# The last norm, gate and output of a fused layer: squares, splits and factors placed sooner, weight remainders read from DRAM, gate operands two steps ahead

## The chip, the cores and the metric

The kernel runs on one core of a Trainium2 chip. The core has five engines that run side by side, each through its own list of instructions in a fixed order: PE (TensorE, the matmuls), DVE (VectorE), ACT (ScalarE), POOL (GpSimd) and SP (SyncE, which here only issues DMAs). The engines wait for each other by semaphores. The metric is the device time of one execution in microseconds, lower is better. Three executions of the kernel before took 2519.19, 2524.06 and 2526.34 us, median 2524.06.

## The reference

One layer on 2048 prompt tokens and 64 further tokens, width 1024, all in float32. What matters for this change is its end; `x` is the layer's input and `p` a side input of width 256:

```python
merged = sigmoid(gA) * yA + sigmoid(gB) * yB
out = einsum('btd,de->bte', merged, w_o)
x = x + rms_norm(out, g_post)
gate = sigmoid(einsum('btd,de->bte', rms_norm(x, g_ple), w_ple_gate))
x = x + einsum('btp,pd->btd', p, w_ple_proj) * gate
```

`rms_norm(x, g)` is `x * rsqrt(mean(x*x) + 1e-6) * g`, the mean over the 1024 features of one token. Everything ahead of it (the input projections, a short convolution, a chunked recurrence) is not touched.

## The kernel before, in words

**Numbers.** A float32 product is made of three matmuls in a rounded format: each operand is split into a high part (a cast, on ACT) and a remainder (a subtraction, on DVE), and PE adds high x high, high x remainder and remainder x high. `split` (L229) is that pair for an activation; `split_w` (L269) does it for a weight tile of 128x512 that SP has loaded (L240). A weight's remainder is the same for every block of tokens, so `split_w` stores it in DRAM the first time and later only loads it (L280, 256 KB, in place of the subtraction); the argument `anew` names the parts that are split again all the same.

**Blocks.** The 2112 tokens go in three blocks of 768, 704 and 640 tokens; features lie on the partitions in eight tiles (j = 0 to 7) of 128, tokens along the row. The last block is worked on in two halves of 320 tokens.

**Products in turn.** Large products of the last block are made by `in_turn` (L573): a 2 x 2 scheme with seven products in place of eight, one after the other, 48 matmuls of 128x320 each (L608, L609, L610). A product's moving operand is half of the activation or a sum of halves (its names are B11, B21, T1 to T4, B22); `operand_of` (L555) makes it from four pieces, k = 0 to 3, each with additions (L559 to L566) and a split (L230). `prepare` asks for the pieces of the next product while the current one runs. Each finished output tile goes to the stage's `sink`.

**The end phase**, which is where the change is, runs after the last product W_O. In order on PE: the seven products of W_O; the final gate of block 2 (704 tokens, W_G: its tiles j = 0 and 1 together, then j = 2 to 7, each 48 matmuls of 128x352, L645 to L647); the `ple` product of block 3 (w_ple_proj, L1313 to L1315); the gate of block 3 as `gate_in_turn` (seven products of W_G, 336 matmuls); and a tail of elementwise work and stores. Block 2's gate is kept back until then so that PE has work while block 3's `final_norm` (L1420) runs on the other engines. That norm is a chain:

- `sum_squares` (L736): eight squares on ACT (L741), summed on DVE (L742).
- `col_rstd` (L713): PE transposes the sum (L722), DVE reduces (L723) and scales (L700), POOL takes the power (L702); then PE transposes the result into rows (L710) and ACT copies it out (L733).
- for each j: scale by g_post (L1446), add `x` that a DMA has fetched (L1431, L1447), and the squares of the second norm.
- the same chain again for the second norm, then one scaling for each j (L1469), which gives the operand of `gate_in_turn`.

Where the chain's PE instructions stand among the gate's matmuls is set by a plan: `spread_out` (L1528) attaches steps of generators to places in the program (a hook after each group of matmuls), and tuples of counts say how many steps each place runs. Of `final_gate` (L1495), each j loads x and p of block 2 again (L1339, on POOL's queue), and makes sigmoid (L1506), product (L1507), sum (L1508) and a store of y (L1509, POOL's queue). Block 2's normed activation h was stored to DRAM (L1478) and is loaded again and split in W_O (`ask_h` L1480, `split_held` L1487).

**Buffers.** Row-shaped tiles (`r_...` in the profile) come from one ring; a new one waits until the last reader of the old one is through. A DMA of POOL also waits until the one eight places earlier in its list has landed.

**The middle block** (block 2 in its own turn, around 1720 to 1780 us) runs the same `final_norm`, but its PE work goes among the gate projections of block 3, and its x is stored to DRAM by POOL (L1457) for the final gate.

Of the kernel before, what the change touches and what calls it, by code (L numbers as in the profile page):

```python
# [14 lines left out]
ALU = mybir.AluOpType  # L15
# [5 lines left out]
KB = D // P  # L21
# [73 lines left out]
def hybrid_step(  # L95
# [474 lines left out]
            V.tensor_tensor(b12, b22, b12, ALU.subtract)  # L570
        return out

    def in_turn(stages, operand):  # L573

# [9 lines left out]
                made.setdefault(i, []).append(operand_of(st["raw"], st["order"][n][1], k, late))  # L584


        for k in range(2):
            prepare(1, k)
        for i, (st, n) in enumerate(todo):
            block, _, what = st["order"][n]  # L590
# [3 lines left out]
            for g in range(KH):  # L594
# [33 lines left out]
                elif what in ("p5", "p7"):  # L628
# [2 lines left out]
                        A.copy(t, ps)  # L631
                    V.tensor_tensor(p57, p57, t, ALU.add)
                    st["sink"](g, 1, 1, u2, p57)
                if i > 0:
                    prepare(i + 1, g)
                elif g < KH - 2:
                    prepare(1, g + 2)
                hook()
# [778 lines left out]
        stage["sink"] = sink  # L1417
        return stage

    def final_norm(bl, xo, acc, kept, take, early):  # L1420

        segs = bl["segs"]
        acc2, xks = None, []

        def fetch():
            j = len(xks)
            if j < KB:
                xks.append(rt())  # L1430
                paced(G.dma_start(xks[j], x_fm[j * P : (j + 1) * P, bl["t0"] : bl["t0"] + bl["n"]]))  # L1431

        for j in range(KB):
            sum_squares(j, xo[j], acc, width[0])
            if j % 2:
                yield
        for _ in range(2):
            fetch()
            yield
        rs = rt()  # L1440
        for _ in rms(acc, rs, segs):
            fetch()
            yield
        for j in range(KB):
            fetch()
            V.scalar_tensor_tensor(xo[j], xo[j], g_post[:, j : j + 1], rs, ALU.mult, ALU.mult)  # L1446
# [5 lines left out]
        stored = iter(range(0 if bl["last"] else KB))  # L1452

        def store(n):
            for i in islice(stored, n):
                kept["x", i] = spill("x", i)
                paced(G.dma_start(kept["x", i], xo[i]))  # L1457

        rs2 = rt()
        for _ in rms(acc2, rs2, segs):  # L1460
            store(2)
            yield
        ts = []
        for j in range(KB):
            store(1)
            while len(ts) < min(j + 1 + early, KB):
                i = len(ts)
                ts.append(rt())
                V.scalar_tensor_tensor(ts[i], xo[i], g_ple[:, i : i + 1], rs2, ALU.mult, ALU.mult)  # L1469
            take(j, ts[j])  # L1470
            yield
# [23 lines left out]
    def final_gate(bl, h2, kept, by_k=False):  # L1495

        segs = bl["segs"]
        for j in range(KB):
            if by_k and j < 2:
                both = gemm_by_k([W_G, W_G + 1], h2, segs, (1,)) if j == 0 else both  # L1500
                pss = both[j]
            else:
                pss = gemm(W_G + j, h2, segs, (1,) if by_k else ())
            xj, pj, t = reload(kept["x", j]), reload(kept["p", j]), rt()
            for s, ps in zip(segs, pss):
                A.activation(t[:, cols_of(s)], ps, AF.Sigmoid)  # L1506
            V.tensor_tensor(t, pj, t, ALU.mult)  # L1507
            V.tensor_tensor(t, t, xj, ALU.add)  # L1508
            G.dma_start(y_fm[j * P : (j + 1) * P, bl["t0"] : bl["t0"] + bl["n"]], t)  # L1509
            yield  # L1510

    def gate_in_turn(bl, h2, xs, kept):


        def sink(g, c, h, x, y):
# [5 lines left out]
            (V if (c, h) == (0, 1) else G).tensor_tensor(v, v, half(xs[j], h), ALU.add)  # L1521
# [148 lines left out]
    for bi, bl in enumerate(blocks):  # L1670
# [78 lines left out]
        for idx, n in in_turn(stages, a_first):  # L1749
# [2 lines left out]
                ask_rs()  # L1752
            elif nxt and (idx, n) == (W_B, 6):
                spread_out((next_ops(), (0, 1, 0, 1, 0, 1, 0) * KH))
            elif bl["last"] and idx == W_O and 1 <= n <= 4:
                run(asked, 2)
            elif bl["last"] and (idx, n) == (W_O, 5):
                a_first.clear()
                norm = sized(bl, final_norm(bl, xo, rt(), kept, lambda j, t: h2.append(t), 0))
                spread_out(  # L1760
                    (held_parts, (1,) * 4 + (2, 2)),
                    (norm, (0,) * 4 + (1,) * 4 + (2, 1, 0, 1, 1, 1, 2, 1, 2, 1, 1, 0) + (1, 1, 2, 1, 2, 1, 1)),
                    (sized(bl, ask_p()), (0,) * 16 + (1, 0, 0, 1)),
                    (sized(bl, first_halves()), (0,) * 24 + (1,) * 4),
                )
        if nxt:
            xo.extend(stages[-1]["mid"])
            fills = sized(nxt, gates(nxt, hc, kepts[bi + 1], False))
            norm = sized(bl, final_norm(bl, xo, rt(), kept, partial(split_h, h2) if first else partial(keep_h, kept), int(first)))
# [8 lines left out]
        else:  # L1778
# [55 lines left out]
```

## Time and profile before

| what | value |
|---|---|
| runs | 2519.19, 2524.06, 2526.34 us; median 2524.06 |
| profiled execution | 2522.08 us, of which the span from the first to the last instruction is 2520.4 us |
| PE busy | 2495.2 us, 99% of the span, 16254 matmuls |
| DVE, ACT, POOL busy | 1943.3 (77%), 1504.2 (60%), 530.9 us (21%) |
| DMA | 741.95 MB, mean 294 GB/s |
| end phase | gate of block 2 from 2374.19, W_G in turn from 2458.79, last matmul begins 2513.52 |

Times inside the kernel are in us from the span's start. In a row of the timeline stand the start, the duration, the engine and line, the operation with its written and read tiles, and, in brackets, how long the engine had been idle and which instruction ended that. A row of the waits names the waiting engine and line, the one it waited for, and total, count and longest. The windows give each engine's busy time within a stretch, the clock that PE was granted (1.00 is full speed) and the busy share and rate of the DMA engines. "PEld" is the loading of weights into PE, which runs beside matmuls.

### The profile page before, as it was taken

Reading aid. Unit: us, or ns where it says so; the run is one execution under the profiler, and the core shown is the slowest. Engines: PE = TensorE matmul, PEld = TensorE weight load, DVE = VectorE, ACT = ScalarE, POOL = GpSimd, SP = SyncE. Lnnn points to the kernel's source line nnn. Section 1 sums busy time; section 2 is a strip of 40 time slices with the busy share of each in tenths; the row PEclk is TensorE's granted clock in tenths of the full one; section 3 lists DMA queues with packets and bytes.
Section 4 is the critical chain, followed back from the end, with each engine's and each line's share of the span. In section 5 each row is a group of like instructions: output and inputs, shape, how many; then the busy total and the mean of one; then the engine's idle time right before and its main releaser. Section 6 shows DMA issues by size and latency. Waiting matters only on the chain. (4 is left out here: it accounts for less than half of the span.)

```text
span 2520.4 us, 47301 instructions
## 1 busy us (share of the span) xinstructions
PE 2495.2 (99%) x16254; PEld 2476.1 (98%) x16254; DVE 1943.3 (77%) x3699; ACT 1504.2 (60%) x2926; POOL 530.9 (21%) x891
## 2 busy tenths in 40 slices
PE   9999999999999999999999999999999999999998
PEld 9999999999999999999999999999999999999998
DVE  7889999988867775588885667977677776679667
ACT  6676676554554763566555555676666655566645
POOL 2032222320022021122223221002122222110133
PEclk9999999999999999999999999999999999999999
DMA  8789889997687798788889988989988879888876
GB/s 330 241 305 338 313 297 324 330 318 266 231 334 263 258 330 292 255 272 284 280 282 332 336 299 310 323 272 355 329 285 290 276 260 324 279 304 307 292 250 212
DMA packets 341937, 741.95 MB, mean 294 GB/s; under 512 B 43062, under 2 KB 48240, under 8 KB 341696
## 3 DMA queue, kind: packets, MB, share of 16 engines
q1 hardware_dynamic: 284832, 515.76, 59.1%
q0 software_dynamic: 56864, 223.16, 24.8%
q8 instruction: 128, 2.10, 0.3%
q14 instruction: 113, 0.93, 0.1%
HBM read 526.40 MB, written 212.36 MB: 293 GB/s over the span
## 5 line engine op out<-in xcount | busy, mean ns | idle before, releaser
L457 PE MATMUL pg<-r,hi 128*128 128x320 f32 (+2 forms) x3304 | 1074.7, 325 | 1.7 <-DVE r L505 1.7
L458 PE MATMUL pg<-r,hi 128*128 128x320 f32 (+2 forms) x3304 | 1066.8, 323 | 0.0
L459 PE MATMUL pg<-r,lo 128*128 128x384 f32 (+2 forms) x2380 | 775.3, 326 | 0.0
L457 PEld LDWEIGHTS pg<-r,hi 128*128 128x128 f32 x3304 | 621.0, 188 | 4.0 <-DVE r L505 2.2
L458 PEld LDWEIGHTS pg<-r,hi 128*128 128x128 f32 x3304 | 621.6, 188 | 0.0
L279 ACT CAST hi<-raw 128x512 fp32r<-128x512 f32 x550 | 339.9, 620 | 407.7 <-PE pg L458 158.8
L459 PEld LDWEIGHTS pg<-r,lo 128*128 128x128 f32 x2380 | 447.1, 188 | 0.3 <-DMA lo<-low 0.3
L230 ACT CAST hi<-raw 128x512 fp32r<-128x512 f32 x420 | 259.4, 621 | 219.8 <-PE pg L458 81.0
L609 PE MATMUL pg<-r,hi 128*128 128x320 f32 (+2 forms) x976 | 313.3, 322 | 1.6 <-DVE r L230 1.5
L608 PE MATMUL pg<-r,hi 128*128 128x320 f32 (+2 forms) x976 | 310.4, 321 | 1.4 <-ACT r L230 1.4
L459 PE MATMUL pg<-r,s 128*128 128x352 f32 (+1 forms) x924 | 291.5, 315 | 2.1 <-DMA s<-low 2.1
L230 DVE TENSOR_TENSOR lo<-raw,hi 128x512 fp32r<-128x512 f32 x320 | 219.4, 687 | 93.5 <-ACT hi L230 88.6
L230 DVE TENSOR_TENSOR r<-r,r 128x320 fp32r<-128x320 f32 (+7 forms) x374 | 221.0, 611 | 44.1 <-ACT r L230 43.3
L230 ACT CAST r<-r 128x320 fp32r<-128x320 f32 (+7 forms) x374 | 195.9, 557 | 34.1 <-DVE r L1353 8.8
L610 PE MATMUL pg<-r,lo 128*128 128x320 f32 (+2 forms) x656 | 209.2, 319 | 0.0
L609 PEld LDWEIGHTS pg<-r,hi 128*128 128x128 f32 x976 | 183.9, 189 | 4.1 <-DVE r L230 3.8
L608 PEld LDWEIGHTS pg<-r,hi 128*128 128x128 f32 x976 | 182.9, 188 | 3.3 <-ACT r L230 2.9
L230 ACT CAST hi<-s 128x512 fp32r<-128x512 f32 x164 | 101.9, 623 | 126.9 <-PE pg L458 99.0
L459 PEld LDWEIGHTS pg<-r,s 128*128 128x128 f32 x924 | 173.5, 188 | 2.4 <-DMA s<-low 2.4
L471 ACT COPY hf<-pg 128x352 f32<-128x352 f32 (+2 forms) x354 | 157.5, 448 | 0.8 <-PE pg L459 0.7
L230 DVE TENSOR_TENSOR lo<-s,hi 128x512 fp32r<-128x512 f32 x164 | 114.1, 696 | 45.0 <-ACT hi L230 40.6
L505 DVE TENSOR_TENSOR r<-hf,pg 128x128 f32<-128x128 f32 (+5 forms) x164 | 64.3, 411 | 95.7 <-PE pg L459 95.4
(391 smaller groups left out, 4239.0 us busy)
## 6 DMA issues: line engine op xcount, KB each, us to landing
raw<-w_blk SPq DMA_DIRECT2D x559, 256.0 KB, 4.5
raw<-S SPq DMA_DIRECT2D x452, 256.0 KB, 4.1
lo<-low SPq DMA_DIRECT2D x332, 256.0 KB, 4.3
s<-low SPq DMA_DIRECT2D x218, 256.0 KB, 4.9
low<-lo SPq DMA_DIRECT2D x207, 256.0 KB, 4.0
S<-s SPq DMA_DIRECT2D x152, 256.0 KB, 4.1
low<-r POOLq DMA_DIRECT2D x66, 256.0 KB, 4.4
r<-w_blk POOLq DMA_DIRECT2D x64, 256.0 KB, 6.6
```

The lines of the kernel that those rows point to most:

```text
L230: return A.copy(hi, src).ins, V.tensor_tensor(lo, src, hi.bitcast(F32), ALU.subtract).ins
L279: A.copy(hi, raw)
L457: add(hi[:, k, :], xhi, start=start and k == 0, stop=False)
L458: add(hi[:, k, :], xlo, start=False, stop=False)
L459: last[0] = add(lo[:, k, :], xhi, start=False, stop=k == KH - 1).ins
L471: copied = A.copy(got[n], ps[bank])
L505: V.tensor_tensor(dst, x, y, ALU.add)
L608: add(hi[:, k, :], xhi, start=start and k == 0, stop=False)
L609: add(hi[:, k, :], xlo, start=False, stop=False)
L610: last[0] = add(lo[:, k, :], xhi, start=False, stop=k == KH - 1).ins
```

## The change

Six things, none of which alters a value that is computed, except for the order in which squares are summed.

1. **W_O**: the loads of h, the hooks and the split of h start one step of W_O earlier, after step 4 in place of step 5.
2. **The last block's norm**: squares are taken in the order j = 4 to 7, 0 to 3, and the plan places the first transposes one gate tile (48 matmuls) earlier. The loads of block 3's p (L1290) are earlier on POOL's list.
3. **Remainders of W_G** in the final gate and in `gate_in_turn` come from DRAM: `anew` is empty. That takes 16 subtractions of 128x512 from DVE and adds 16 loads of 256 KB (SP's list has 1993 rows after, 1977 before).
4. **`in_turn` for W_G with lead 2**: the operand of step 1 is prepared whole before step 0, that of step 2 during step 0, and so on.
5. **The sink of `gate_in_turn`**: 16 multiplications and additions move from POOL to DVE.
6. **The middle block**: its x is stored from the norm's tile j = 4 on, one store for each step, and not from the second set of transposes on.

On PE only the places of the transposes differ. Ahead of this change the first transposes stand behind gate tile j = 2 (tiles `pg_...` are PE's results, `pa_...` those of the transposes, `ident` the unit matrix); with it they stand behind tiles 0 and 1:

Before:

```order
L647 MATMUL pg_30744<-r_30611,lo_30712 128x352
L645 MATMUL pg_30744<-r_30614,hi_30711 128x352
L646 MATMUL pg_30744<-r_30330,hi_30711 128x352
L647 MATMUL pg_30744<-r_30614,lo_30712 128x352
L722 MATMUL pa_30771<-ident,r_30436 128x128 x3
L722 MATMUL pa_30776<-ident,r_30436 128x128 x3
L645 MATMUL pg_30807<-r_30456,hi_30797 128x352
```

After:

```order
L645 MATMUL pg_30568<-r_30626,hi_30561 128x352
L646 MATMUL pg_30568<-r_30242,hi_30561 128x352
L647 MATMUL pg_30568<-r_30626,s_30562 128x352
L722 MATMUL pa_30689<-ident,r_30508 128x128 x3
L722 MATMUL pa_30694<-ident,r_30508 128x128 x3
L645 MATMUL pg_30735<-r_30384,hi_30725 128x352
L646 MATMUL pg_30735<-r_29936,hi_30725 128x352
```

The 48 matmuls of tile 2 now come behind the transposes; the remainder of tile 1's weights is a loaded tile (`s_30562`). The second set of L722 keeps its place.

On DVE, in the early steps of W_G in turn, the operand T2 is made (L562 the sum, L566, L230 the split), and the rows of weights `lo_...<-raw_...` are remainders of weights.

Before:

```order
L230 TENSOR_TENSOR lo_31623<-raw_31620,hi_31622 128x512
L564 TENSOR_TENSOR r_31323<-r_31403,r_31323 128x320
L559 TENSOR_TENSOR r_31348<-r_31348 128x320
L564 TENSOR_TENSOR r_31348<-r_31431,r_31348 128x320
L230 TENSOR_TENSOR lo_31654<-raw_31651,hi_31653 128x512
L562 TENSOR_TENSOR hf_31582<-r_31373,r_31296 128x320
L566 TENSOR_TENSOR r_31373<-r_31373,hf_31582 128x320
L230 TENSOR_TENSOR r_31586<-hf_31582,r_31586 128x320
```

After:

```order
L559 TENSOR_TENSOR r_31296<-r_31296 128x320
L1471 SCALAR_TENSOR_TENSOR r_31429<-r_28390,vec,r_31191 128x640
L230 TENSOR_TENSOR r_31403<-r_31321,r_31403 128x320
L562 TENSOR_TENSOR hf_31496<-r_31373,r_31296 128x320
L564 TENSOR_TENSOR r_31296<-r_31373,r_31296 128x320
L230 TENSOR_TENSOR r_31431<-r_31346,r_31431 128x320
L1471 SCALAR_TENSOR_TENSOR r_31457<-r_28391,vec,r_31191 128x640
```

T2's first sum moves from behind all the splits of weights to between the norm's last scalings (L1471, L1469 before), and the splits of weights are gone.

On POOL, in the middle block, the stores of x (`x_...<-r_...`) stand among the stores of the gate projections (L876).

Before:

```order
L876 DMA g__5017_21704<-r_21525 128x640
L876 DMA g__5056_21879<-r_21709 128x640
L876 DMA g__5055_21877<-r_21708 128x640
L1457 DMA x_22016<-r_20549 128x704
L1457 DMA x_22018<-r_20573 128x704
L702 TENSOR_TENSOR cols_22003<-cols_22003,mhalf 128x6
L876 DMA g__5096_22053<-r_21882 128x640
```

After:

```order
L876 DMA g__5017_21704<-r_21525 128x640
L1431 DMA x_21809<-r_20549 128x704
L1431 DMA x_21843<-r_20573 128x704
L1431 DMA x_21881<-r_20605 128x704
L876 DMA g__5059_21885<-r_21709 128x640
L876 DMA g__5058_21883<-r_21708 128x640
L1431 DMA x_21966<-r_20629 128x704
L1431 DMA x_22024<-r_20435 128x704
L702 TENSOR_TENSOR cols_22011<-cols_22011,mhalf 128x6
```

Five stores of x stand ahead of the power (L702) in place of two.

The diff, cut to its core:

```diff
-    def in_turn(stages, operand):
+    def in_turn(stages, operand, lead=1):
...
-        for k in range(2):
+        for k in range(2 if lead == 1 else KH):
             prepare(1, k)
...
-                if i > 0:
-                    prepare(i + 1, g)
+                if lead > 1 or i > 0:
+                    prepare(i + lead, g)
                 elif g < KH - 2:
                     prepare(1, g + 2)
...
-    def final_norm(bl, xo, acc, kept, take, early):
+    def final_norm(bl, xo, kept, take, early):
...
-        for j in range(KB):
-            sum_squares(j, xo[j], acc, width[0])
-            if j % 2:
+        acc = rt()
+        for i in range(KB):
+            sum_squares(i, xo[(i + KH) % KB if bl["last"] else i], acc, width[0])
+            if i % 2:
                 yield
...
             sum_squares(j, xo[j], acc2, width[0])
+            if j >= KH and not early:
+                store(1)
             yield
...
         for _ in rms(acc2, rs2, segs):
-            store(2)
+            store(1 + early)
             yield
...
-                both = gemm_by_k([W_G, W_G + 1], h2, segs, (1,)) if j == 0 else both
+                both = gemm_by_k([W_G, W_G + 1], h2, segs) if j == 0 else both
...
-                pss = gemm(W_G + j, h2, segs, (1,) if by_k else ())
+                pss = gemm(W_G + j, h2, segs)
...
-            (G if c == h == 0 else V).tensor_tensor(v, v, t, ALU.mult)
-            (V if (c, h) == (0, 1) else G).tensor_tensor(v, v, half(xs[j], h), ALU.add)
+            V.tensor_tensor(v, v, t, ALU.mult)
+            V.tensor_tensor(v, v, half(xs[j], h), ALU.add)
...
-        return dict(idx=W_G, order=IN_TURN, raw=h2, anew=("A11", "A12"), sink=sink)
+        return dict(idx=W_G, order=IN_TURN, raw=h2, anew=(), sink=sink)
...
-            elif bl["last"] and idx == W_O and 1 <= n <= 4:
+            elif bl["last"] and idx == W_O and n < 4:
                 run(asked, 2)
-            elif bl["last"] and (idx, n) == (W_O, 5):
+            elif bl["last"] and (idx, n) == (W_O, 4):
...
-                    (held_parts, (1,) * 4 + (2, 2)),
-                    (norm, (0,) * 4 + (1,) * 4 + (2, 1, 0, 1, 1, 1, 2, 1, 2, 1, 1, 0) + (1, 1, 2, 1, 2, 1, 1)),
...
+                    (held_parts, (0, 1, 0, 1) + (1,) * 6),
+                    (norm, (0,) * 4 + (0, 0, 1, 1) + (1, 3, 0, 1) + (0, 1, 1, 1, 2, 1, 1, 1, 1, 0, 1, 0) + (1, 1, 1, 2, 1, 1, 1, 1)),
...
-            for idx, n in in_turn([gate_in_turn(bl, h2, xo, kept)], a_first):
+            for idx, n in in_turn([gate_in_turn(bl, h2, xo, kept)], a_first, 2):
```

More of the change, by code (lines that the diff above doesn't have):

```diff
@@ L1418, in out_in_turn, with store @@
         return stage
-    def final_norm(bl, xo, acc, kept, take, early):
+    def final_norm(bl, xo, kept, take, early):
         segs = bl["segs"]
         acc2, xks = None, []
+        stored = iter(range(0 if bl["last"] else KB))
+        def store(n):
+            for i in islice(stored, n):
+                kept["x", i] = spill("x", i)
+                paced(G.dma_start(kept["x", i], xo[i]))
         def fetch():
@@ L1450, in final_norm @@
             sum_squares(j, xo[j], acc2, width[0])
+            if j >= KH and not early:
+                store(1)
             yield
[L1452 to L1457, printed above, removed]
         rs2 = rt()
         for _ in rms(acc2, rs2, segs):
-            store(2)
+            store(1 + early)
             yield
@@ L1768, in hybrid_step @@
             fills = sized(nxt, gates(nxt, hc, kepts[bi + 1], False))
-            norm = sized(bl, final_norm(bl, xo, rt(), kept, partial(split_h, h2) if first else partial(keep_h, kept), int(first)))
+            norm = sized(bl, final_norm(bl, xo, kept, partial(split_h, h2) if first else partial(keep_h, kept), int(first)))
             spread_out((norm, (1,) * 6 + (0,) * 5 + (1, 0, 0, 1, 1) + (0, 1) * (KB - 1) + (0, 0, 1, 0, 0, 1) + (1, 0) * (KB - 3) + (1, 1, 1)))
```

6 lines of the change are left out of this document (3 added, 3 removed).

## The prediction

> **What bounds the kernel now.** I read the page's busy times first, then what PE waited for, then five-microsecond windows of the end phase, and last the timeline of each stretch in which PE lost time. The page:
>
> ```profile
> span 2520.4 us, 47301 instructions
> PE 2495.2 (99%) x16254; PEld 2476.1 (98%) x16254; DVE 1943.3 (77%) x3699; ACT 1504.2 (60%) x2926; POOL 530.9 (21%) x891
> ```
>
> PE is the bound: 25.2 us of the span are not PE's. The change takes no matmul away, so all it can win is idle time of PE, time in which PE runs at a lower clock, and the tail. What PE waits for, longest first, with what belongs to the places of the change:
>
> ```profile
> PE pa L722 <- DVE r L742: 3.6, 1, 3.6
> PE pg L459 <- DMA s<-low: 2.1, 1, 2.1
> ...
> PE pg L609 <- DVE r L230: 1.5, 3, 0.9
> PE pg L608 <- ACT r L230: 1.4, 2, 0.9
> ...
> PE pg L645 <- ACT hi L279: 0.5, 1, 0.5
> ...
> PE pg L610 <- DMA s<-low: 0.3, 1, 0.3
> ```
>
> One wait of 3.6 us is the second norm's transposes waiting for the sum of squares. The windows add what waits don't show, the granted clock (the number behind PE's, PEld's, DVE's, ACT's and POOL's busy time; then DMA share and GB/s):
>
> ```profile
> 1740.00:1770.00 30.00, 30.00 (x210) 29.98 (x209) 16.96 (x30) 15.72 (x31) 11.12 (x19) 1.00 1.03 393
> 1770.00:1775.00 5.00, 2.86 (x19) 2.60 (x19) 1.92 (x3) 1.26 (x2) 1.61 (x3) 1.00 1.03 400
> ...
> 2440.00:2445.00 5.00, 5.00 (x29) 5.00 (x29) 2.60 (x6) 1.18 (x3) 1.36 (x2) 0.86 0.46 165
> 2475.00:2480.00 5.00, 2.79 (x12) 2.07 (x12) 4.96 (x6) 2.46 (x7) 4.23 (x6) 0.89 0.53 200
> 2480.00:2485.00 5.00, 5.00 (x29) 5.00 (x29) 4.28 (x11) 3.84 (x10) 0.52 (x1) 0.77 0.77 245
> 2485.00:2510.00 25.00, 25.00 (x172) 25.00 (x172) 13.47 (x30) 16.52 (x37) 9.91 (x13) 1.00 0.75 250
> ```
>
> There are two bad places in the end phase, around 2435 (the wait of L722) and 2475, and each is followed by some microseconds at a lower clock (0.86 and 0.77) in which a fully busy PE does 29 matmuls where 34 fit. 2485 to 2510 is the undisturbed case: 172 matmuls in 25 us, 0.147 us each.
>
> **The change, part by part.**
>
> *Gate of block 2, start.* Its two stalls are the rows of L645 and L610 above, 0.5 and 0.3 us. One waited for a cast queued behind the splits of h, the other for a remainder from DRAM. With h's loads and splits a step of W_O (48 matmuls, 7 us) sooner both go: gain 0.75 us (0 to 0.8).
>
> *First norm.* These rows of the timeline show its chain, DVE's last sums, PE's two sets of transposes, POOL's power and DVE's first scaling:
>
> ```profile
> 2382.71 2.69 DVE L742 TENSOR_TENSOR r<-r,r 128x640 f32<-128x640 f32 x3 [0.46 <-ACT hi L279]
> 2398.07 0.81 PE L722 MATMUL pa<-ident,r 128*128 128x128 f32 x6
> 2400.52 1.35 POOL L702 TENSOR_TENSOR cols<-cols,mhalf 128x6 f32<-128x6 f32 x1 [0.91 <-DVE cols L700]
> 2406.45 0.82 PE L710 MATMUL pa<-ident,cols 128*128 128x128 f32 x6
> 2409.26 1.68 DVE L1446 SCALAR_TENSOR_TENSOR r<-r,vec,r 128x640 f32<-128x640 f32 x2
> ```
>
> The sum is ready at 2385.40, 12.7 us before its transposes stand in PE's order. They now come 48 matmuls earlier, 7.7 us at the 0.16 us of these matmuls, so 5 us of slack are left even if the squares came no sooner. The power ends 4.6 us before L710; both move together. Cost nothing, while the sum covers it; its effect is that L1446 and all behind it may start about 8.4 us sooner (7.7 and the 0.75).
>
> *Second norm.* The wait and what follows it on PE:
>
> ```profile
> 2436.91 0.83 DVE L742 TENSOR_TENSOR r<-r,r 128x640 f32<-128x640 f32 x1 [0.80 <-ACT r L741]
> ...
> 2437.89 1.47 PE L722 MATMUL pa<-ident,r 128*128 128x128 f32 x6 [3.60 <-DVE r L742]
> ...
> 2439.01 0.64 PE L645 MATMUL pg<-r,hi 128*128 128x352 f32 x1
> ...
> 2441.45 0.32 PE L647 MATMUL pg<-r,lo 128*128 128x352 f32 x1
> 2441.61 0.32 PE L645 MATMUL pg<-r,hi 128*128 128x352 f32 x1
> ```
>
> L722 could have begun at 2434.29 and keeps its place in PE's order, so it comes due at 2433.5. The last sum of squares ended at 2437.74; 8.4 us sooner is 2429.3, with 4.2 us to spare. The 3.6 us go. So does the slow stretch: between 2439.01 and 2441.45 lie 8 matmuls (2.44 us against 8 x 0.16 = 1.28, or 1.2 lost), and the six transposes took 1.47 where the first set took 0.81, of which I count 0.5. Together 5.3 us (0 to 5.3; less than nothing if a new wait takes its place, which is the first rival).
>
> *Gate in turn.* Step 2 of the seven lost nearly all of what this product lost:
>
> ```profile
> 2458.79 0.30 PE L608 MATMUL pg<-r,hi 128*128 128x320 f32 x1
> ...
> 2470.01 1.02 POOL L1521 TENSOR_TENSOR r<-r,r 128x320 f32<-128x320 f32 x1
> 2470.20 1.17 DVE L562 TENSOR_TENSOR hf<-r,r 128x320 f32<-128x320 f32 x1
> 2471.41 0.49 DVE L566 TENSOR_TENSOR r<-r,hf 128x320 f32<-128x320 f32 x1
> 2471.90 1.27 DVE L230 TENSOR_TENSOR r<-hf,r 128x320 fp32r<-128x320 f32 x1
> ...
> 2513.52 0.31 PE L610 MATMUL pg<-r,lo 128*128 128x320 f32 x1
> ```
>
> From the first to the last of the 336 matmuls pass 54.73 us; 335 x 0.147 is 49.2. The loss is 5.5 us: four waits for T2's pieces (the 1.4 and 1.5 us of the second fence, nearly all here) and the slow clock of the window of 2480. T2 is late because DVE reaches it at 2470 and because its L562 and L230 take 1.2 us while POOL multiplies and adds, where L566 of the same shape takes 0.49.
>
> Afterwards DVE makes T2 with 36 instructions from the norm's first last scaling to T2's last split: 8 scalings of 128x640 at 0.84 (L1446's row, two in 1.68) and 28 of 128x320 at 0.49, 20.4 us. The second power would end near 2437.4, L710 comes due near 2439.9, the copy is done near 2442.3, so T2 is whole by 2462.7. W_G starts at 2458.79 - 6.0 = 2452.7 and step 2 at 2452.7 + 96 x 0.147 = 2466.8: 4 us to spare. Gain 5.5 us (0 to 5.5).
>
> A rule bears on how the slow stretches are counted. The Trainium skill, "TensorE: Matmul & The Clock Gate", section "What's actually happening", has PE's clock halve after an idle window of about 3.4 us. By it the 3.6 us wait costs clock and the 2.1 us one of the middle block doesn't, as the windows have it (0.86 behind the one, 1.00 beside the other), but gaps below 0.9 us as in step 2 should not, and 1.5 us of the 5.5 would then stay. The window of 2480 has 0.77 behind just these gaps, so the trace decides and I count the whole.
>
> *What the moved work costs.* DVE loses 16 subtractions and gets 16 operations of 128x320; the first were 0.69 us each:
>
> ```profile
> L230 DVE TENSOR_TENSOR lo<-raw,hi 128x512 fp32r<-128x512 f32 x320 | 219.4, 687 | 93.5 <-ACT hi L230 88.6
> ...
> lo<-low SPq DMA_DIRECT2D x332, 256.0 KB, 4.3
> ```
>
> That is 11.0 us out and 7.8 in, so DVE is relieved; within W_G it is 5.5 out and 7.8 in, 2.3 us more in a product whose later 25 us leave DVE idle for 11.5. POOL is rid of them. The 16 loads (4.2 MB) land in 4.3 us; seven buffers rotate for them, each read by 12 matmuls, so a load has up to 12 us. The whole of W_G needs 28 weight tiles and 28 remainders of 256 KB and 16 stores of 160 KB, 17.3 MB in 49.2 us or 351 GB/s if nothing were fetched ahead, where the window of 1740 shows 393 over 30 us. Cost nothing (0 to 8 us if only 300 GB/s were to be had, 57.6 us).
>
> *Tail.* PE's last matmul begins at 2513.52, and the last tile's sum is made late:
>
> ```profile
> 2514.62 0.49 DVE L1521 TENSOR_TENSOR r<-r,r 128x320 f32<-128x320 f32 x1
> 2515.03 0.48 DVE L498 TENSOR_TENSOR hf<-r,pg 128x320 f32<-128x320 f32 x1
> ```
>
> L498 stood behind the addition of the tile ahead; now it stands before it. Gain 0.5 us (0 to 0.6).
>
> *Middle block.* Its stall is the 2.1 us at L459, when a remainder's load is late in a stretch with the DMA engines full (the windows of 1740 and 1770, share 1.03). Eight stores of 352 KB by POOL lie in it; the first begins 108 matmuls (15.9 us) sooner now, five stand ahead of the power. They move 1.4 MB, 3.6 us at 393 GB/s, out of the full stretch, but the stretch before it is nearly full too:
>
> ```profile
> 1725.00:1740.00 15.00, 15.00 (x104) 15.00 (x103) 14.57 (x23) 11.12 (x21) 1.07 (x2) 1.00 0.91 328
> ```
>
> With 9% of 15 us it has 1.35 us spare. I take 1.3 us (2.1 gained to 1 lost, the latter if a remainder is late there instead).
>
> *Sum.* 0.75 + 5.3 + 5.5 + 0.5 + 1.3 = 13.35 us. The profiled execution took 2522.08 us, 1.7 us over its span and 2.0 under the median of 2524.06. It would take 2508.7, and against the median the forecast is 2510.7, say 2511 us.
>
> **The rivals.**
>
> *A new wait at the second L710 (no change).* The reductions of the second norm (L723) now stand on DVE behind the product and sum of gate tile 6, and these need a p that POOL loads. POOL's rounds of load, product, store were long:
>
> ```profile
> 2401.84 0.60 POOL L1339 DMA_DIRECT2D r<-p  x1
> 2406.92 0.89 DVE L1507 TENSOR_TENSOR r<-r,r 128x704 f32<-128x704 f32 x1 [6.49 <-DMA r<-p]
> 2410.92 0.55 POOL L1339 DMA_DIRECT2D r<-p  x1
> 2421.32 0.55 POOL L1339 DMA_DIRECT2D r<-p  x1
> ```
>
> Rounds of 9.1 and 10.4 us. The first p behind a store of y is that of tile 2; it should land near 2408, 1 us later than in the trace. From there p of each tile stands behind the store of the tile two before it (that of tile 6 behind y of tile 4, where it was behind y of tile 5), so two rounds lead to tile 6. At 11.5 us each, DVE being busier, p lands at 2431.4, its product and sum end at 2433.2, ahead of the transposes, and the power ends 2.5 us before L710. Three rounds of 10.4 in place of two give 2439.5, then 1.8 us of product and sum and 3.3 from L723 to the power's end, 2444.6: a stall of 4.7 us and 1.7 of slow clock, 2517. Four rounds (each tile waits for the one ahead of it, as in the trace) give 2449.9, a stall of 15 us and 2527. For this speaks that the chain hangs on POOL's list and the margin is 2.5 us; against it, the list itself.
>
> *The same, worse (slower).* From four rounds of 11.5 us on, L710 is held for 19.2 us or more and the result is over 2531.6, slower by 0.3%. DVE's busier list speaks for longer rounds; the two that the rows show are 9.1 and 10.4.
>
> *T2 is late still (faster, by less).* If L562 and L230 keep 1.2 us, eight of them add 5.6 us, T2 ends at 2468.3, PE waits 1.5 us and perhaps 2 at a low clock: 2514.5. Against it, POOL has no product or sum left there.
>
> *Part of it doesn't work.* The norm's chain is no sooner, for x's reloads now stand behind three fetches and the first power on POOL's list; then 5.3 us stay and the result is 2516 to 2519.
>
> **How the numbers follow.** 0.3%, 7.6 us, is about what a measurement of this kernel can tell from no change. The forecast (2506 to 2515) gets 0.62; T2 late 0.10; the new wait 0.14, of which 0.03 stays faster; part not working 0.08, 0.03 of it faster; slower 0.06. Faster: 0.62 + 0.10 + 0.06 = 0.78. Same: 0.11 + 0.05 = 0.16. Slower: 0.06. The range runs from 2504 (the full sum, the stall of the middle block gone whole, and a run as low as the lowest shown stands to its median) to 2520, with part of the new wait; above it lies some 0.15.
>
> **What would show it.** Right: no wait of L722 on L742 in PE's list, clock 1.00 from 2430 to 2445 and through W_G, W_G's matmuls within 50 us, L562 and L230 at 0.49 us, PE idle 12 us less. Wrong: a wait of L710 on POOL's power or of DVE's product on p of tile 6; waits of L610 or L647 on remainders from DRAM; a new stall of L459 between 1725 and 1770.

## The result

The changed kernel takes 2509.44 us (median of six runs, 2505.88 to 2510.86) against 2523.1 us of the kernel before (six runs, the three of above among them): a ratio of 0.9945, 95% interval 0.9932 to 0.9958, 13.7 us less. Forecast were 2511 us. In a later set beside the kernel before the same code had 0.9938 (0.9925 to 0.9952). The profiled execution took 2510.86 us, 11.2 less than the one of before. Its page and PE's waits:

```profile
span 2509.2 us, 47311 instructions
PE 2491.1 (99%) x16254; PEld 2474.0 (99%) x16254; DVE 1932.2 (77%) x3699; ACT 1503.9 (60%) x2926; POOL 513.9 (20%) x875
```

```profile
PE pg L609 <- DVE r L230: 2.5, 4, 0.9
PE pa L722 <- DVE r L742: 1.3, 1, 1.3
```

PE is the bound as before, now with 18.1 us of the span not its own (25.2 before). Neither row is of the end phase: the 1.3 us are in the middle block at 1742, and 2.0 of the 2.5 us lie at 2272 to 2277, in code that the change doesn't touch. The windows of the places that were bad in the end phase:

```profile
2430.00:2440.00 10.00, 10.00 (x68) 9.97 (x67) 4.94 (x8) 3.81 (x11) 3.51 (x5) 1.00 0.93 303
2440.00:2450.00 10.00, 10.00 (x71) 10.00 (x70) 7.69 (x11) 7.47 (x20) 0.60 (x1) 1.00 0.86 293
2470.00:2480.00 10.00, 10.00 (x70) 10.00 (x69) 4.40 (x11) 6.03 (x15) 0.33 (x1) 1.00 1.02 365
2480.00:2490.00 10.00, 10.00 (x70) 10.00 (x69) 5.10 (x12) 5.73 (x13) 1.51 (x3) 1.00 0.93 306
```

PE is busy without a gap and at full clock in all of them. The timeline of the changed kernel, the rows that answer to those of the prediction (line numbers are some lines higher here; L1453 was L1446, L1509 was L1507, L1523 was L1521):

```profile
2389.67 0.81 PE L722 MATMUL pa<-ident,r 128*128 128x128 f32 x6
2400.70 1.67 DVE L1453 SCALAR_TENSOR_TENSOR r<-r,vec,r 128x640 f32<-128x640 f32 x2
2428.12 0.82 DVE L742 TENSOR_TENSOR r<-r,r 128x640 f32<-128x640 f32 x1 [0.87 <-ACT r L741]
2433.41 0.82 PE L722 MATMUL pa<-ident,r 128*128 128x128 f32 x6
2433.56 0.89 DVE L1509 TENSOR_TENSOR r<-r,r 128x704 f32<-128x704 f32 x1 [1.51 <-DMA r<-p]
2436.60 1.35 POOL L702 TENSOR_TENSOR cols<-cols,mhalf 128x6 f32<-128x6 f32 x1
2439.70 0.82 PE L710 MATMUL pa<-ident,cols 128*128 128x128 f32 x6
2452.68 0.31 PE L608 MATMUL pg<-r,hi 128*128 128x320 f32 x1
2462.31 0.48 DVE L230 TENSOR_TENSOR r<-hf,r 128x320 fp32r<-128x320 f32 x1
2502.05 0.30 PE L610 MATMUL pg<-r,lo 128*128 128x320 f32 x1
```

The second norm's sum is ready at 2428.94, 4.5 us ahead of its transposes; the power ends 1.75 us ahead of L710; T2's last split ends at 2462.79; and W_G's 336 matmuls take 49.4 us from first to last, where they took 54.7.

Counted by stretches, this trace is shorter than that of before by 6.1 us from the first matmul of block 2's gate to W_G's first (78.5 us, 84.6 before), by 5.4 us in W_G, and longer by 0.3 us from W_G's last matmul to the end. Up to the gate the two traces take the same time: it begins at 2374.21 here and at 2374.19 before. That is a chance of these two traces. With the new stores of the middle block the gate begins between 2369.07 and 2374.21 in nine traces (median 2372.36), with the old ones between 2373.46 and 2378.04 in five (median 2374.19).

### The profile page after: what moved, and what is told of

It is laid out like the page before. It is cut to its first block, busy times and chain, and to the rows that moved or that the text cites. A ratio compares the mean times of both kernels' runs of the same rounds, so it can differ in the third digit from the quotient of the medians.

```text
span 2509.2 us, 47311 instructions
## 1 busy us (share of the span) xinstructions
PE 2491.1 (99%) x16254; PEld 2474.0 (99%) x16254; DVE 1932.2 (77%) x3699; ACT 1503.9 (60%) x2926; POOL 513.9 (20%) x875
## 4 chain that ended last, share of the span: by engine, by line
PE 90%; DMA 3%; DVE 3%; ACT 2%; issue 1%; POOL 0%; SPq 0%; ACTq 0%; DVEq 0%; POOLq 0%
PE pg L457 20%; PE pg L458 19%; PE pg L459 19%; PE pg L609 5%; PE pg L608 5%; PE pg L610 5%; PE pg L646 3%; PE pg L647 3%; PE pg L645 3%; DMA raw<-S 2%; PE pa L1142 1%; PE pa L1110 1%; PE pa L1180 1%; PE pa L1182 1%; DMA raw<-w_blk 1%
## 5 line engine op out<-in xcount | busy, mean ns | idle before, releaser
L459 PE MATMUL pg<-r,lo 128*128 128x384 f32 (+2 forms) x2380 | 775.3, 326 | 0.4 <-DMA lo<-low 0.4
L459 PEld LDWEIGHTS pg<-r,lo 128*128 128x128 f32 x2380 | 447.1, 188 | 0.7 <-DMA lo<-low 0.7
L230 ACT CAST hi<-raw 128x512 fp32r<-128x512 f32 x404 | 249.5, 621 | 206.3 <-PE pg L458 83.8
L609 PE MATMUL pg<-r,hi 128*128 128x320 f32 (+2 forms) x976 | 312.1, 321 | 2.5 <-DVE r L230 2.5
L608 PE MATMUL pg<-r,hi 128*128 128x320 f32 (+2 forms) x976 | 309.8, 320 | 0.0
L459 PE MATMUL pg<-r,s 128*128 128x352 f32 (+1 forms) x924 | 291.4, 315 | 0.0
L230 DVE TENSOR_TENSOR lo<-raw,hi 128x512 fp32r<-128x512 f32 x304 | 208.1, 686 | 82.7 <-ACT hi L230 75.9
L230 DVE TENSOR_TENSOR r<-r,r 128x320 fp32r<-128x320 f32 (+7 forms) x374 | 220.2, 608 | 46.1 <-ACT r L230 44.9
L230 ACT CAST r<-r 128x320 fp32r<-128x320 f32 (+7 forms) x374 | 195.9, 557 | 35.0 <-DVE r L1353 9.0
L609 PEld LDWEIGHTS pg<-r,hi 128*128 128x128 f32 x976 | 183.2, 188 | 4.6 <-DVE r L230 4.3
L608 PEld LDWEIGHTS pg<-r,hi 128*128 128x128 f32 x976 | 182.3, 188 | 1.4 <-ACT r L230 1.0
L230 ACT CAST hi<-s 128x512 fp32r<-128x512 f32 x164 | 101.9, 623 | 127.3 <-PE pg L458 97.0
L459 PEld LDWEIGHTS pg<-r,s 128*128 128x128 f32 x924 | 173.5, 188 | 0.0
L230 DVE TENSOR_TENSOR lo<-s,hi 128x512 fp32r<-128x512 f32 x164 | 114.2, 696 | 45.6 <-ACT hi L230 43.1
```

Source lines behind the costliest of these rows:

```text
L230: return A.copy(hi, src).ins, V.tensor_tensor(lo, src, hi.bitcast(F32), ALU.subtract).ins
L459: last[0] = add(lo[:, k, :], xhi, start=False, stop=k == KH - 1).ins
L608: add(hi[:, k, :], xhi, start=start and k == 0, stop=False)
L609: add(hi[:, k, :], xlo, start=False, stop=False)
```

## The experiments

Every kernel was timed beside the kernel before on its chip, in five rounds or more; the ratio is to that. 0.001 is 2.5 us.

| label | what it is | median us | ratio, 95% interval |
|---|---|---|---|
| changed_again | the changed kernel | 2506.74 | 0.9938 (0.9925 to 0.9952) |
| lead_one | changed, lead 1 | 2507.35 | 0.9942 (0.9929 to 0.9954) |
| pool_sink | changed, sinks on POOL | 2508.19 | 0.9942 (0.9930 to 0.9955) |
| lead_one_pool | changed, both of these | 2513.92 | 0.9963 (0.9950 to 0.9977) |
| splits_back | changed, remainders made by DVE | 2513.19 | 0.9965 (0.9953 to 0.9978) |
| plan_old | changed, old places of the norm | 2516.98 | 0.9978 (0.9969 to 0.9987) |
| only_plan | before, new places of the norm | 2521.98 | 0.9999 (0.9990 to 1.0008) |
| only_loads | before, remainders loaded | 2525.23 | 1.0010 (1.0001 to 1.0018) |
| only_dve_sink | before, sinks on DVE | 2518.26 | 0.9984 (0.9975 to 0.9992) |
| middle_old | changed, old stores of the middle block | 2510.83 | 0.9954 (0.9941 to 0.9966) |
| tail_sp | changed, last four stores on SP | 2506.55 | 0.9934 (0.9922 to 0.9947) |
| tail_sp_more | changed, last eight stores on SP | 2505.73 | 0.9934 (0.9920 to 0.9947) |

**Why step 2 of W_G was late.** Three kernels undo the two parts that concern it, alone and together.

```diff
-            for idx, n in in_turn([gate_in_turn(bl, h2, xo, kept)], a_first, 2):
+            for idx, n in in_turn([gate_in_turn(bl, h2, xo, kept)], a_first):
```

> The changed kernel with lead 1: the operand of a step of W_G is prepared one step ahead, as before the change; everything else as changed. My theory is that step 2 was late because DVE reached T2 late. With lead 1 the four pieces of T2 are made between the products and sums of step 1's output, about 20 operations of 0.42 us from 2462, so the last piece is ready near 2469 where step 2 needs it near 2468: a wait of about 1 us and some slow clock, 1 to 3 us longer than the changed kernel, some 2511. The rival, that the sinks on POOL alone made T2 late, expects no loss at all (2509.4), since POOL runs none here.

```diff
-            V.tensor_tensor(v, v, t, ALU.mult)
-            V.tensor_tensor(v, v, half(xs[j], h), ALU.add)
+            (G if c == h == 0 else V).tensor_tensor(v, v, t, ALU.mult)
+            (V if (c, h) == (0, 1) else G).tensor_tensor(v, v, half(xs[j], h), ALU.add)
```

> The changed kernel with the 16 products and sums of the gate's output back on POOL, lead 2 kept. My theory: T2 is whole near 2462.8, before POOL's first product, so no wait of step 2 returns: within 1 us of the changed kernel (2509 to 2510.5), although DVE's operations beside POOL's take 1.2 us again in place of 0.49. The rival, that the contention with POOL was what cost the 5.5 us, expects them back: 2515.

Both edits together:

> The changed kernel with lead 1 and the sinks on POOL: both parts undone that concern step 2, the weights' remainders still from DRAM. My theory: T2's pieces are made from 2462 on beside POOL's products, about 2.9 us each, so the waits of step 2 return, with the slow clock behind them: 4 to 6 us longer, 2513.5 to 2515.5. The rival, that it was the eight splits of weights in W_G that made T2 late, expects no loss (2509.4).

Either part alone is enough: `lead_one` (where I had expected to lose 1 to 3 us) and `pool_sink` can't be told from the changed kernel, and neither has a wait of PE in W_G, which takes 49.7 and 49.4 us. With both undone it takes 55.4 us, and the median is 5.7 to 6.6 us longer than with one, on the same chip. The timeline of `lead_one_pool`, DVE making T2 and PE in step 2:

```profile
2462.51 1.16 DVE L562 TENSOR_TENSOR hf<-r,r 128x320 f32<-128x320 f32 x1
...
2464.20 1.27 DVE L230 TENSOR_TENSOR r<-hf,r 128x320 fp32r<-128x320 f32 x1
...
2467.11 0.41 PE L608 MATMUL pg<-r,hi 128*128 128x320 f32 x1 [0.56 <-ACT r L230]
...
2468.40 0.41 PE L609 MATMUL pg<-r,hi 128*128 128x320 f32 x1 [0.88 <-DVE r L230]
...
2469.97 0.64 PE L608 MATMUL pg<-r,hi 128*128 128x320 f32 x1 [0.86 <-ACT r L230]
```

These are the rows of the kernel before again, and its eight splits of weights in W_G are not there: the loss doesn't need them. With lead 2 the same contention exists but comes after T2, as the timeline of `pool_sink` shows:

```profile
2460.47 0.49 DVE L230 TENSOR_TENSOR r<-hf,r 128x320 fp32r<-128x320 f32 x1
...
2461.18 0.87 POOL L1522 TENSOR_TENSOR r<-r,hf 128x320 f32<-128x320 f32 x1 [19.94 <-ACT hf L1520]
...
2482.81 0.88 POOL L1523 TENSOR_TENSOR r<-r,r 128x320 f32<-128x320 f32 x1 [10.13 <-DVE r L1522]
2482.96 0.49 DVE L498 TENSOR_TENSOR hf<-r,pg 128x320 f32<-128x320 f32 x1 [0.24 <-PE pg L610]
```

T2's last split is done 0.2 us before POOL's first product. The last two rows tell which operations of DVE suffer: L498, which reads one tile from SBUF and one from PSUM (`pg`), takes its usual 0.49 us beside a POOL sum, where L562 and L230, with both inputs in SBUF, take 1.16 and 1.27. The Trainium skill, "SBUF — State Buffer", section "SBUF: two separate sides", says just this: VectorE and GpSimd share a port pair that the one or the other holds for a whole instruction, and a VectorE operation needs it when it has two SBUF inputs while GpSimd reads SBUF. These rows agree.

The kernel before with the sinks moved alone (the same two lines, the other way):

> The kernel before with only the 16 products and sums moved from POOL to DVE. My theory: T2's operations take 0.49 us in place of 1.2, but DVE still reaches T2 near 2470 and the products and sums now stand between its pieces, so its last split ends near 2478.6 in place of 2481: 1 to 3 us less than the kernel before, the tail's 0.5 included. The rival, that contention with POOL was the whole cause, expects 5.5 to 6 us less.

The wait of step 2 is gone although DVE still comes late to T2:

```profile
PE pa L722 <- DVE r L742: 4.4, 1, 4.4
...
PE pg L609 <- DVE r L230: 0.2, 1, 0.2
```

It gained 4.0 us (0.0016), more than my 1 to 3 and less than the rival's 5.5 to 6. In its trace W_G takes 49.8 us, 5.0 less than before, and the wait of L722 is 0.8 us longer. So the contention by itself was the cause, and DVE's late start on T2 did next to no harm without it (0.4 us against the changed kernel's W_G).

**Why the second norm's wait went.** Remainders made by DVE again:

```diff
-        return dict(idx=W_G, order=IN_TURN, raw=h2, anew=(), sink=sink)
+        return dict(idx=W_G, order=IN_TURN, raw=h2, anew=("A11", "A12"), sink=sink)
...
-                pss = gemm(W_G + j, h2, segs)
+                pss = gemm(W_G + j, h2, segs, (1,) if by_k else ())
```

> The changed kernel with the weights' remainders made by DVE again (8 in the gate of block 2, 8 in W_G), no added loads; lead 2 and the sinks on DVE kept. My theory: 8 x 0.6 us put the second norm's last sum from 2429 to at most 2434, where L722 comes due at 2434.0, and T2 from 2462.8 to 2467.6, where step 2 begins at 2466.8: 0 to 2 us longer, 2509 to 2511.5. A rival in which the 16 loads cost DMA time expects this kernel faster than the changed one, by up to 2 us.

By the ratios it lost 5 to 7 us against the changed kernel, not 0 to 2. In its list POOL issues the loads of x and p of gate tile 6 behind the store of y of tile 5, as the kernel before does, and no longer behind that of tile 4. Its waits of PE, then DVE's product of tile 6 and POOL's rows:

```profile
PE pa L710 <- POOL cols L702: 2.9, 1, 2.9
```

```profile
2420.99 0.54 POOL L1511 DMA_DIRECT2D y_fm<-r  x1 [3.12 <-DVE r L1510]
2426.33 0.54 POOL L1511 DMA_DIRECT2D y_fm<-r  x1 [4.79 <-ACT r L1508]
2426.86 0.55 POOL L1339 DMA_DIRECT2D r<-x  x1
2427.40 0.55 POOL L1339 DMA_DIRECT2D r<-p  x1
...
2432.90 0.89 DVE L1509 TENSOR_TENSOR r<-r,r 128x704 f32<-128x704 f32 x1 [5.67 <-DMA r<-p]
```

DVE stands still for 5.67 us for that p, with the reductions of the norm (L723) behind it. This is the mechanism of the prediction's first rival, one store later in place of one round later.

My expectation laid a loss to the time of the splits on DVE, and the trace doesn't bear that out. Counted from the gate's first matmul (2369.35 here, 2374.21 in the changed kernel), y of tile 4 is issued after 51.6 us here and after 52.9 there, y of tile 5 after 57.0 and 58.4: with its splits DVE is no later. What the edit cost in this trace is the place that the loads of tile 6 take in POOL's list, which changed with it. No run changes that list alone.

The norm's places, undone and alone:

```diff
-            elif bl["last"] and idx == W_O and n < 4:
+            elif bl["last"] and idx == W_O and 1 <= n <= 4:
...
-            elif bl["last"] and (idx, n) == (W_O, 4):
+            elif bl["last"] and (idx, n) == (W_O, 5):
...
-                    (held_parts, (0, 1, 0, 1) + (1,) * 6),
+                    (held_parts, (1,) * 4 + (2, 2)),
```

(and the other plans and the order of the squares likewise)

> The changed kernel with the old places of the last norm: loads and splits of h a step of W_O later, squares in the order 0 to 7, first transposes behind gate tile 2. The remainders still come from DRAM, lead 2 and the sinks on DVE stay. My theory: the norm's chain moves back by some 8 us, so the wait of L722 for the second sum returns in part (before it was 3.6 us; six splits of weights fewer stand in DVE's list ahead of that sum, at most 3.6 us), with slow clock behind it: 2 to 5 us longer than the changed kernel, which stands 13.7 us under the kernel before. The rival, that the splits of weights alone made the norm late, expects no loss.

`only_plan` is the kernel before with these lines as changed:

> The kernel before with only the new places of the last norm (and h's loads and splits a step of W_O sooner). My theory: 0.75 us at the gate's start and the 3.6 us wait with its 1.7 us of slow clock would go, 6 us in all; but the run with the splits brought back showed that eight splits on DVE make a wait of 2.9 us at the second L710, and these stand here too. I expect 1 to 4 us less than the kernel before, with that wait in the trace, and the 5.5 us of W_G untouched. The rival, that the places alone are enough, expects 6 us less.

`only_loads` is the kernel before with `anew` empty:

> The kernel before with only the 16 remainders of W_G loaded in place of made. My theory: the wait of 3.6 us at the second L722 shrinks by up to 3.6 us, since six splits of 0.6 us leave DVE's list ahead of the second sum; where DVE waited for p the split cost nothing, so I expect 1 to 3 us of it. In W_G T2 is reached some 4 us sooner but is still made beside POOL's products, so 0 to 3 us of its 5.5 go. In all 1 to 6 us less than the kernel before. The rival, that the added 4.2 MB delay other loads, expects no gain and waits for DMA in PE's list.

PE's waits in `plan_old`, in `only_plan` and in `only_loads`:

```profile
PE pa L722 <- DVE r L742: 4.1, 1, 4.1
PE pa L710 <- POOL cols L702: 1.3, 1, 1.3
```

```profile
PE pa L710 <- POOL cols L702: 5.8, 1, 5.8
```

```profile
PE pa L722 <- DVE r L742: 3.3, 1, 3.3
...
PE pa L710 <- POOL cols L702: 1.4, 1, 1.4
```

Undone, the places cost 8 to 10 us by the ratios, more than the 2 to 5 I expected. Alone they gained nothing: L722 waits no more, L710 waits 5.8 us, and the rival of 6 us fell with my own 1 to 4. The loads alone gained nothing either (0.3 us off one wait, 1.4 on another), and I had expected 1 to 6 us.

From the gate's first matmul to W_G's first the kernel before takes 84.6 us, `only_loads` 86.3, `plan_old` (the loads, old places) 86.8, `only_plan` 87.6, `splits_back` (the places, no loads) 83.2 and the changed kernel 78.5. So the two parts work only together: the places bring the sum in time, and with the loads as well POOL's list has p of tile 6 a store sooner, which brings the reductions behind it in time. (`splits_back` and `only_plan` have the same order here; what differs is how soon the loads land, p of tile 3 after 5.1 us in the one and 7.8 in the other, each in a single trace.)

**The middle block.** The old stores of x:

```diff
-            if j >= KH and not early:
-                store(1)
...
-            store(1 + early)
+            store(2)
```

> The changed kernel with the stores of the middle block's x where they were before. My theory: the wait of L459 for a remainder from DRAM near 1770 returns, 1.7 to 2.4 us in the traces of the kernels with the old stores and absent in five of the six with the new: 2 us longer than the changed kernel on the same chip. The rival, that the wait comes and goes by chance and is not bound to the stores, expects no difference and a trace without the wait.

> The changed kernel itself, beside the one with the old stores of the middle block on the same chip. My theory: 13 to 14 us under the kernel before, no wait of PE between 1720 and 1800, and none of the 2.0 us at L609 that its first trace had near 2273 for a late load of weights. If that wait was part of the change it stands here again.

The old stores bring the wait back; the timeline of `middle_old`:

```profile
1773.70 0.42 PE L459 MATMUL pg<-r,lo 128*128 128x320 f32 x1 [1.74 <-DMA lo<-low]
...
1777.35 0.41 PE L459 MATMUL pg<-r,s 128*128 128x320 f32 x1 [1.61 <-DMA s<-low]
```

All five traces with the old stores have waits of L459 here, 1.8 to 3.4 us in all. Of the nine with the new stores eight have PE busy for all of 1720 to 1800, and one, the first of the changed kernel, has the 1.3 us at L722. The first store of x is issued at 1725.63 in the changed kernel's first trace, 16.2 us sooner than before, and the stretch that had 0.91 of the DMA engines' time busy now has 0.98:

```profile
1725.00:1740.00 15.00, 15.00 (x105) 15.00 (x104) 13.46 (x21) 9.99 (x20) 3.23 (x6) 1.00 0.98 358
```

The medians of `middle_old` and `changed_again` are 4.1 us apart, with intervals that overlap. `changed_again` has no wait in 2272 to 2277, and neither has any other trace with the change, so that one of the first trace was chance.

**The tail.** In the traces the span ends 6.91 to 6.98 us after POOL's last store begins to be issued (7.31 in `only_plan`), while from DVE's last sum to the end it is 3.2 us with the sinks on POOL and 4.6 with them on DVE. POOL's last store before, and in the changed kernel:

```profile
2513.42 0.54 POOL L1523 DMA_DIRECT2D y_fm<-r  x1 [0.21 <-issue]
```

```profile
2502.23 0.54 POOL L1525 DMA_DIRECT2D y_fm<-r  x1 [0.95 <-DVE r L1523]
```

The kernel's last line holds the closing instructions of each engine, a DRAIN the first of them on POOL. The rows of that line for POOL's and SP's queues give the count, the shortest, median and longest duration in ns, and the first and last start; first before, then in the changed kernel:

```profile
L1825 POOLq DRAIN  x3: 40/102/6194, 2513.4 to 2520.1; - x3
L1825 SPq DRAIN  x3: 7/7/7, 2519.4 to 2519.9; - x3
```

```profile
L1827 POOLq DRAIN  x3: 40/93/6192, 2502.2 to 2508.9; - x3
L1827 SPq DRAIN  x3: 7/7/7, 2506.9 to 2508.7; - x3
```

POOL's first DRAIN begins with its last store and takes 6.19 us; from its end to the span's end it is 0.8 us in both. SP is through its closing waits, the last store among them, at 2519.4 before, 0.2 us ahead of the end of POOL's DRAIN, and at 2506.9 in the changed kernel, 1.5 us ahead of it. So a shorter chain on DVE had nothing to win while that store came no sooner, and the end came 0.3 us later behind the last matmul: POOL's last store is issued 0.10 us before the last matmul begins in the kernel before and 0.18 us after it in the changed one, where it waits for DVE's sum.

```diff
-            (SP if (c, h) == (0, 1) and g >= 2 else G).dma_start(y_fm[...], v)
+            (SP if (c, h) == (0, 1) else G).dma_start(y_fm[...], v)
```

> The changed kernel with the four stores of the last output tiles all on SP's queue (two of them were on POOL's). In the traces so far the span ends 6.91 to 6.98 us after POOL's last store begins to be issued (7.31 in one), while the time from DVE's last sum to the end varies from 3.2 to 4.6: so the end seems to hang on POOL's last store. My theory now: POOL's last store is issued some 2.7 us earlier, and the end comes 1.5 to 2.7 us sooner after PE's last matmul (7.1 us in the changed kernel, then 4.4 to 5.6). The rival, that DVE's last sum and the last store on SP set the end, expects 7.1 as before.

With `in ((0, 1), (1, 1))` in place of `== (0, 1)`:

> As the run before, with the four stores of the step ahead on SP as well, so that POOL's last store lies another 8 us back and only SP's queue can set the end. My theory: no sooner than the run before, since there SP's last store already sets the end: the same time from PE's last matmul to the end within 0.3 us. If the end still hung on POOL there, it comes sooner again here.

PE's last matmul in `tail_sp` and in `tail_sp_more`, whose spans are 2506.2 and 2503.5 us:

```profile
2500.71 0.30 PE L610 MATMUL pg<-r,lo 128*128 128x320 f32 x1
```

```profile
2498.19 0.30 PE L610 MATMUL pg<-r,lo 128*128 128x320 f32 x1
```

From there to the end pass 5.5 and 5.3 us, 7.15 in the changed kernel: 1.6 us are won, and a second step wins 0.2 more, within the 0.3 expected. POOL's DRAIN is over 2.0 us ahead of the end in `tail_sp` and 10.5 us in `tail_sp_more`; the end hangs on SP there. These two are the shortest kernels of the study by ratio, 16.7 us under the kernel before, but their intervals overlap with the changed kernel's; what is shown is the 1.6 us of the trace.

## Why the prediction was right, point by point

- *What bounds the kernel, and that only gaps and clock could be won*: right. The end phase has no wait of L722, L710, L608 or L609 left. The sign "PE idle 12 us less" was set too high: some 4 us of the forecast were slow clock, in which PE is busy, and PE's idle time fell by 7.1 us.
- *Gate start, 0.75 us*: right; PE is busy for all of 2370 to 2380 in the changed kernel's trace.
- *First norm, no cost*: right. L722 came 15.5 us after the gate's start (23.9 before), L1453 8.56 us sooner (forecast 8.4).
- *Second norm, 5.3 us*: right in size, and the times were met (sum at 2428.94 against 2429.3, L722 at 2433.41 against 2433.5). The reason given, that the chain starts sooner and "The 3.6 us go", was half of it. `only_plan` shows that the places alone only move the wait to L710. The loads in place of splits, which the prediction entered as relief for DVE at no gain, are the other half; the order of POOL's list, which the prediction took as given in its first rival, hangs on them.
- *The rival of the second L710*: it didn't come, and its margin was as thin as said (1.75 us, forecast 2.5). p of tile 6 landed at 2433.5, 2 us later than worked out.
- *The times met to 0.1 us* (L722, W_G's start, T2's end): partly luck. They are reckoned from the trace of before without the 1.3 us forecast ahead of the gate, and fit because both traces begin the gate at 2374.2; `changed_again` begins it at 2369.07. What was right are the distances from the gate's start.
- *Gate in turn, 5.5 us*: right (5.4). Of the two reasons given, the late start of DVE and POOL's contention, only the second was a cause by itself; and two parts of the change each removed it.
- *How the slow clock is counted*: the trace's way was right; the gaps of step 2 brought the clock down again in `lead_one_pool`, `only_plan` and `only_loads`. That the 2.1 us wait of the middle block costs no clock holds for the trace of before, not in general: one of 2.18 us at the same place did in `only_loads`, and the last section shows what decides. (Of the two windows in which "34 fit", that of 2440 has matmuls of 0.16 us, of which 31 fit.)
- *Tail, 0.5 us*: wrong, the step that failed. The last tile's sum is indeed made 1.0 us sooner after the last matmul, but the end is 7.15 us behind that matmul, 6.88 before. I took DVE's chain for the end. It was POOL's last store with the DRAIN behind it, and the moved sums made that store 0.3 us later.
- *Middle block, 1.3 us*: the mechanism was right, the size uncertain: by the waits 0.8 us in the first trace, 2 us and more in the others, and 1.8 us by the medians of the gate's start.
- *The moved work at no cost*: right for the 16 loads, no remainder was late.

The sum of 13.35 us against 13.7 measured by the medians is closer than its terms. The two profiled executions differ by 11.2 us, all of it behind the gate's start, where 12.05 were forecast; the tail gave nothing, and the part ahead of the gate differs from trace to trace by more than was forecast for it. The range's lower edge, 2504, lies 1 us under what its terms give (2510.7 less 0.8 and 4.9).

## What to carry to other kernels

A wait that ends a chain is worth its full length only when every link behind it is early too; ask of each moved step what stands behind the moved instruction in the other engines' lists, here a reduction behind a product that waited for a reload. Count times from a point just ahead of the change, since a time from the program's start holds all that differs before. Two small repairs of one spot don't add up, and two links of one chain don't pay singly: try a change's parts alone and together before keeping or dropping any. And look for what the end of the program is tied to, by constant distances over several traces and by the closing rows of every engine, before shortening the chain that seems to end last.

## What the runs showed of the hardware

**The clock.** Up to the last matmul a lowered clock lasts 3.41 us, or twice that (in `lead_one_pool` and behind the wait of 5.8 us in `only_plan`), and it can begin after the wait is over. The timeline of `only_loads`, PE around the second transposes:

```profile
2437.97 0.84 PE L722 MATMUL pa<-ident,r 128*128 128x128 f32 x6 [3.29 <-DVE r L742]
...
2439.15 0.42 PE L645 MATMUL pg<-r,hi 128*128 128x352 f32 x1
...
2442.59 0.36 PE L645 MATMUL pg<-r,hi 128*128 128x352 f32 x1
```

After 3.29 us of waiting the transposes still ran at full clock (0.84 us for six; 1.47 in the kernel before); the slow matmuls are those from 2439.15 to 2442.59, 3.4 us. The Trainium skill, "TensorE: Matmul & The Clock Gate", section "What's actually happening", has the clock set by a free-running window of 3.4 us; the length and the delay agree. That a single idle stretch of a window is needed doesn't agree: three waits of at most 0.88 us within 3.4 us were enough in `lead_one_pool`, while two of 1.74 and 1.61 us, 3.65 us apart, left the clock at 1.00 in `middle_old`.

What decides can be read from the traces. In each of them all changes of the clock up to the last matmul lie on one grid of 3.41 us. Windows on that grid, in `lead_one_pool` (PE's busy time is the first number behind the comma, the granted clock the third from the end):

```profile
2465.92:2469.34 3.42, 1.75 (x9) 1.00 (x7) 3.39 (x4) 1.31 (x3) 2.75 (x4) 1.00 0.95 343
2469.34:2472.75 3.41, 2.78 (x9) 2.53 (x10) 3.38 (x6) 2.31 (x6) 2.99 (x4) 0.50 0.30 107
2472.75:2476.16 3.41, 3.41 (x14) 3.41 (x14) 2.83 (x7) 2.27 (x6) 0.06 (x1) 0.50 0.85 229
```

and in `middle_old`:

```profile
1775.89:1779.31 3.42, 1.96 (x13) 1.96 (x14) 0.08 (x1) 1.16 (x3) 1.60 (x3) 1.00 1.05 403
1779.31:1782.72 3.41, 3.41 (x25) 3.41 (x24) 1.39 (x2) 2.35 (x7) 0.54 (x1) 1.00 1.01 405
```

PE idle for 1.67 us of the first of these windows is followed by half clock, idle for 1.46 us by full clock. Over all 14 traces, each of the 11 full-clock windows with 1.67 us or more of idle PE is followed by one at 0.50, and none with 1.61 us or less. So it is the idle share of a window on the grid, a little under a half, and a wait counts by how the grid cuts it: of the 2.18 us wait in `only_loads` 2.06 us lie in one window (it ends at 1773.64) and the clock falls, while in the kernel before a border at 1772.35 cuts the 2.14 us into 1.04 and 1.10, and it doesn't. No run varied a wait for the purpose; the border is read from these traces alone.

**The end.** In every trace POOL's first closing DRAIN begins within 0.3 us of its last store's issue and takes 5.9 to 6.2 us, where a last store on SP allows the end 2.7 to 2.9 us behind DVE's last sum. Why the DRAIN takes so long isn't shown.
